# Queries, keys and rotary keys of the attention kept in DRAM as high and low parts

## The chip, the cores and the metric

The kernel runs on one core of a Trainium2 chip: a matrix engine (TensorE, PE), three others that compute (VectorE or DVE, ScalarE or ACT, GpSimd or POOL), one that mostly issues transfers (SyncE or SP), and 16 DMA engines between DRAM and the core's memory. Each engine works through its own list of instructions in order; semaphores tie the lists together. The metric is the device time of one execution in microseconds (us), smaller is better.

## What is computed

One layer of a diffusion backbone over 512 latent and 256 context tokens of width 2,048. The input projection's columns feed two groups of heads: latent attention, and a bidirectional RWKV-7 recurrence. Then one output projection and a mixture of 32 experts. The change concerns three results of the projection that the attention reads much later:

```
h = modulate(x, norm_attn_g, sh1, sc1)
cq, ckv, kr, r, k, v, wl, al, gl = project_in(h, w_in, shift_mu)
q  = rms_norm(cq,  q_norm_g)  @ w_uq        # cq: 512 wide, 512 tokens
kv = rms_norm(ckv, kv_norm_g) @ w_ukv       # ckv: 256 wide, 768 tokens
k_rope = rope_2d(kr)                        # kr: 64 wide, 768 tokens
g = sigmoid(gl) @ gate_up                   # gate of the RWKV output
```

Matrix products are taken in three passes over operands that are split into a high part (a cast to a shorter format, `fp32r`) and a low part (what is left), so that the sum has nearly float32 precision.

## The kernel before

`layer` is one long program whose instructions a scheduler orders by priority; buffers come from pools, and a pool's memory can be given to the next one only when everything that reads or writes it is done. DMAs raise one of eight semaphore slots, dealt in turn to the DMAs of SP and ACT together; a DMA that gets a slot first waits until the DMA that had it before has landed. So the order in which DMAs are scheduled ties the queues of SP and ACT to each other.

The stages, by the profile's clock: modulation and the first projection columns (to about 155 us); the other projection columns with the norms of queries and keys, the rotation of the rotary key and the gate (to about 294); the RWKV features, feature block by feature block and direction by direction (300 to 880), with POOL solving small triangular systems in the background (`solve`, whose results go out as `r_tt` and `r_tn` on SP); from 820 on the attention (`mla`), interleaved with the recurrence's chain; routing; and from about 1,690 the experts, whose weights stream in.

What the change touches:

- L384 to L400 normalise the queries `cqT` and store them, four DMAs to `r_cq` (float32). L426 to L443 do it for the keys `ckvT` in two ranges of tokens, four DMAs to `r_ckv`. L444 and L445 rotate and store `krT` to `r_kr`.
- Between them L409 to L425 load `gate_up` and split it and the gate's inputs into buffers named `ld`, of which there are three; the loop L446 to L455 forms the gate and stores it, eight DMAs to `r_g`.
- All this lies in the pool `p0` on one side of the memory. When it closes, the RWKV stage's buffers take its place: first the memset of `W` (L551), then `km`, `ks` and others.
- In `mla`, L986 to L989 load the seven pieces on ACT's queue into four buffers `p` and split each: a cast on ACT (L170) and a subtraction on DVE (L171), into `ckn`, `krr` and `cqn`. Behind them on ACT's queue come the weights of the first pair of heads (`load_pair`, L997, L998, L1003, L1004), the copy `p<-pqr` (L1015) of the first rotary queries, and its rotation.

`split(hi, lo, src)` is `sc.copy(hi, src)` and `ve.tensor_sub(lo, src, hi)`.

Of the kernel before, what the change touches and what calls it, by code (L numbers as in the profile page):

```python
# [21 lines left out]
T = 512  # L22
# [58 lines left out]
def layer(ctx, tc, tab, x, c, ctx_in, c_ctx, w_mod, b_mod, norm_attn_g, norm_ffn_g, w_in, shift_mu,  # L81
# [25 lines left out]
    r_cq = dram.tile([4, 128, T], F32, name="r_cq")  # L107
    r_ckv = dram.tile([2, 128, NT], F32, name="r_ckv")
    r_kr = dram.tile([128, NT], F32, name="r_kr")
# [176 lines left out]
    with tc.tile_pool(name="p0", bufs=1, side="right") as p0:  # L286
# [97 lines left out]
        for src, n, dst, g, width, a, b in ((cqT, 4, r_cq, qg, 512.0, 0, 512),):  # L384
            m = b - a
            pn = bank("nq", [128, 512], "rw", 2)[:, 0:m]
            for i in range(n):
                sc.activation(nsq[:, 0:m], src[:, i, a:b], AF.Square)
                te.matmul(pn, ones, nsq[:, 0:m], start=(i == 0), stop=(i == n - 1))
            v, r, u = nv[:, 0:m], nr[:, 0:m], nu[:, 0:m]  # L390
            ve.tensor_scalar(v, pn, 1.0 / width, EPS, op0=OP.mult, op1=OP.add)
            sc.activation(r, v, AF.Sqrt)
            ve.reciprocal(r, r)
            ve.tensor_mul(u, r, r)
            ve.tensor_mul(u, u, v)
            ve.tensor_scalar(u, u, -0.5, 1.5, op0=OP.mult, op1=OP.add)
            ve.tensor_mul(r, r, u)
            for i in range(n):
                ve.scalar_tensor_tensor(src[:, i, a:b], src[:, i, a:b], g[:, i:i + 1], r, op0=OP.mult, op1=OP.mult)
                sy.dma_start(dst[i, :, a:b], src[:, i, a:b])  # L400
# [25 lines left out]
        for src, n, dst, g, width, a, b in ((ckvT, 2, r_ckv, kvg, 256.0, 0, 512),  # L426
                                            (ckvT, 2, r_ckv, kvg, 256.0, 512, 768)):
# [13 lines left out]
            for i in range(n):  # L441
                ve.scalar_tensor_tensor(src[:, i, a:b], src[:, i, a:b], g[:, i:i + 1], r, op0=OP.mult, op1=OP.mult)
                sy.dma_start(dst[i, :, a:b], src[:, i, a:b])  # L443
        rope(krT[:, 0:T], "rw", 2, nsq)  # L444
        sy.dma_start(r_kr, krT)  # L445
        for f in range(NF):  # L446
# [8 lines left out]
            sy.dma_start(r_g[f], g_)  # L455
        early = [project([(3904, 128)], 128)]
# [517 lines left out]
    def mla():  # L974
        with tc.tile_pool(name="mla", bufs=1) as ml:
# [9 lines left out]
            for dst, src, n in ([([t_[:, i] for t_ in ckn], r_ckv[i], NT) for i in range(2)] + [(krr, r_kr, NT)] +  # L985
                                [([t_[:, i] for t_ in cqn], r_cq[i], T) for i in range(4)]):  # L986
                t_ = mt("p", [128, NT], bufs=4)[:, 0:n]
                sc.dma_start(t_, src)
                split(dst[0], dst[1], t_)  # L989
# [700 lines left out]
```

## Time and profile before

| | us |
|---|---|
| time, median of 3 runs | 2669.04 (2664.29 to 2672.88) |
| the profiled execution | 2665.13 |
| its span, first to last instruction | 2663.3 |
| PE busy | 2411.0 (91%) |
| DVE busy | 1406.2 (53%) |
| ACT busy | 914.1 (34%) |
| POOL busy | 737.8 (28%) |
| mean TensorE clock granted, share of full | 0.948 |

The profile shows one execution. Its page gives each engine's busy time and, in 40 slices of 66.6 us, busy tenths; the trace can be asked for an engine's timeline (start, duration, engine, line, operation, output<-input; in brackets how long the engine sat idle before and what released it), for busy times by stretch, and for transfers. A line starting with `SPq` or `ACTq` is a DMA being issued, not moved.

### The profile page before, as it was taken

What the parts mean: (1) busy time and instruction counts of PE and PEld (TensorE: products, weight loads), DVE (VectorE), ACT (ScalarE), POOL (GpSimd) and SP (SyncE); (2) the same over time, 40 slices, a digit from 0 to 9 for tenths busy, and PEclk for the clock granted to TensorE, in tenths of its full rate; (3) what the DMA queues carried; (4) which work ended last, traced back from release to release, by engine and by line L of the source; (5) the groups of instructions that cost most, each with busy time, mean ns of one, the idle gap of its engine ahead of it and who ended that gap; (6) DMA issues with size and microseconds to landing.
All of it is one profiled execution on the core that took longest, in us unless ns stands there. A gap on an engine that the chain in (4) does not pass through costs nothing. (4 is left out here: it accounts for less than half of the span.)

```text
span 2663.3 us, 39444 instructions
## 1 busy us (share of the span) xinstructions
PE 2411.0 (91%) x15238; PEld 1535.9 (58%) x15238; DVE 1406.2 (53%) x2094; ACT 914.1 (34%) x1659; POOL 737.8 (28%) x830
## 2 busy tenths in 40 slices
PE   4999899998997789998968997999999999999995
PEld 2567678887876667777736785434333334334332
DVE  3345687666778767666458545243333334334324
ACT  4245564332333256554534332311111112112202
POOL 1046654016677544554535300000000000000000
PEclk9999999998997789999989997999999999999998
DMA  8965577665667768788687532999999999999995
GB/s 307 345 189 173 190 195 185 135 141 131 150 136 183 175 180 224 223 243 237 189 271 216 193 131 106 411 421 421 421 421 420 418 421 420 420 416 417 420 421 212
DMA packets 521998, 727.50 MB, mean 273 GB/s; under 512 B 320792, under 2 KB 399536, under 8 KB 471376
## 3 DMA queue, kind: packets, MB, share of 16 engines
q1 hardware_dynamic: 410512, 578.97, 62.0%
q0 software_dynamic: 24208, 83.50, 9.5%
q10 hardware_dynamic: 87088, 62.48, 8.1%
q8 instruction: 121, 1.98, 0.3%
q14 instruction: 69, 0.57, 0.1%
HBM read 659.69 MB, written 73.54 MB: 275 GB/s over the span
## 5 line engine op out<-in xcount | busy, mean ns | idle before, releaser
L523 POOL TENSOR_TENSOR scr<-scr 128x512 f32<-128x512 f32 x240 | 327.7, 1365 | 350.5 <-ACT scr L521 331.2
L174 PE MATMUL acc<-hT,w 128*128 128x512 f32 (+1 forms) x752 | 268.7, 357 | 13.0 <-DVE km L276 9.9
L175 PE MATMUL acc<-hT,w 128*128 128x512 f32 (+1 forms) x752 | 268.9, 358 | 0.0
L176 PE MATMUL acc<-hT,w 128*128 128x512 f32 (+1 forms) x752 | 268.3, 357 | 0.0
L1455 POOL DMA_INDIRECT xg<-r_x,ix x16 | 19.1, 1196 | 831.1 <-DVE sp L1440 627.3
L521 ACT ACTIVATE scr<-scr,scl 128x512 f32<-128x512 f32 x256 | 170.4, 715 | 174.8 <-DMA scr<-in_w_mod_dram 140.6
L1600 PE MATMUL py<-ew,gT 128*64 128x512 f32 x680 | 213.8, 607 | 7.9 <-ACT gT L1580 6.7
L1500 DVE TENSOR_TENSOR xm<-xm,pox 128x512 f32<-128x512 f32 x256 | 161.4, 682 | 62.1 <-PE pox L1499 61.5
L171 DVE TENSOR_TENSOR w<-wraw,w 128x512 fp32r<-128x512 f32 (+1 forms) x132 | 110.8, 845 | 140.8 <-ACT w L170 139.7
L1575 DVE SCALAR_TENSOR_TENSOR scr<-ph,ga,scr 128x512 f32<-128x512 f32 x16 | 12.0, 751 | 310.4 <-PE ph L1556 310.4
L1490 DVE TENSOR_TENSOR yt<-py,g2r 128x512 f32<-128x512 f32 x64 | 42.7, 687 | 242.1 <-PE py L1600 228.7
L174 PEld LDWEIGHTS acc<-hT,w 128*128 128x128 f32 (+1 forms) x752 | 144.5, 192 | 36.2 <-issue 15.4
L176 PEld LDWEIGHTS acc<-hT,w 128*128 128x128 f32 (+1 forms) x752 | 143.9, 191 | 22.4 <-issue 1.4
L175 PEld LDWEIGHTS acc<-hT,w 128*128 128x128 f32 (+1 forms) x752 | 144.5, 192 | 20.4 <-issue 1.0
L170 ACT CAST w<-wraw 128x512 fp32r<-128x512 f32 (+1 forms) x132 | 80.5, 613 | 217.7 <-PE acc L175 125.3
L1600 PEld LDWEIGHTS py<-ew,gT 128*64 128x64 f32 x680 | 73.5, 138 | 125.7 <-issue 109.2
L519 POOL DMA_DIRECT2D scr<-in_w_mod_dram x128 | 92.9, 726 | 173.7 <-DVE scr L358 140.7
L170 ACT CAST yr<-yt 128x512 fp32r<-128x512 f32 x64 | 39.3, 619 | 294.3 <-DVE yt L1490 293.0
L479 POOL TENSOR_TENSOR scr<-scr 128x31 f32<-128x31 f32 (+15 forms) x155 | 108.5, 700 | 27.7 <-DMA scr<-r_ab 16.0
L480 POOL TENSOR_TENSOR scr<-scr 128x31 f32<-128x31 f32 (+15 forms) x155 | 108.1, 697 | 12.1
L1498 PE MATMUL pox<-yr,ohT 128*128 128x512 f32 x256 | 105.6, 428 | 4.1 <-ACT yr L170 3.8
L1572 ACT ACTIVATE scr<-ph 128x512 f32<-128x512 f32 x16 | 9.6, 597 | 260.2 <-PE ph L1556 260.2
(702 smaller groups left out, 5381.9 us busy)
## 6 DMA issues: line engine op xcount, KB each, us to landing
ew<-in_w_dram SPq DMA_DIRECT2D x279, 1024.0 KB, 19.8
Y<-in_w_dram SPq DMA_DIRECT2D x70, 1024.0 KB, 19.5
scr<-in_w_mod_dram POOLq DMA_DIRECT2D x128, 512.0 KB, 5.3
scr<-in_w_dram SPq DMA_DIRECT2D x34, 1024.0 KB, 19.8
ld<-in_w_mod_dram SPq DMA_DIRECT2D x32, 1024.0 KB, 7.3
wraw<-in_w_in_dram ACTq DMA_DIRECT2D x104, 256.0 KB, 3.5
wor<-in_w_out_dram ACTq DMA_DIRECT2D x64, 256.0 KB, 3.3
QXr<-r_qx SPq DMA_DIRECT2D x24, 512.0 KB, 6.0
```

What stands on the lines that cost most here:

```text
L170: sc.copy(hi, src)
L171: (lo_eng or ve).tensor_sub(lo, src, hi)
L174: te.matmul(out, lhs[0], rhs[0], start=first, stop=False)
L175: te.matmul(out, lhs[0], rhs[1], start=False, stop=False)
L176: te.matmul(out, lhs[1], rhs[0], start=False, stop=last)
L479: e.tensor_mul(z, xs.to_broadcast([128, n, m]), ms.to_broadcast([128, n, m]))
L480: e.tensor_add(xo, xo, z)
L521: sc.mul(wt[:, k] if kt + k else macc, wt[:, k], scl[:, kt + k:kt + k + 1])
L523: gp.tensor_add(macc, macc, wt[:, k])
L1498: te.matmul(po, ohT[0:np_, 128 * i:128 * i + 128], yr[0], start=True, stop=False)
L1500: ve.tensor_add(xm[:, i, ns], xm[:, i, ns], po)
L1600: te.matmul(pys[n][64 * e:64 * e + 64], gT[:, j, 64 * e:64 * e + 64], ws[e][:, n], start=(j == 0), stop=(j == 3))
```

## The change

`r_cq`, `r_ckv` and `r_kr` get a leading dimension of two. A new function `keep` splits a whole tensor into two of the `ld` buffers and stores both with one DMA each: the queries right after their norm, the keys and the rotary key behind the gate loop. `mla` loads the parts straight into the buffers that the matmuls read: six DMAs, no split. The bytes stored and the bytes loaded both double, from 2.2 to 4.4 MB.

```diff
-        for src, n, dst, g, width, a, b in ((cqT, 4, r_cq, qg, 512.0, 0, 512),):
+        for src, n, g, width, a, b in ((cqT, 4, qg, 512.0, 0, 512),):
...
-                sy.dma_start(dst[i, :, a:b], src[:, i, a:b])
+
+        def keep(dst, src):
+            hl = [p0.tile([128, 4, 512], F32R, name="ld", bufs=3) for _ in range(2)]
+            hl = [t_.rearrange("p a b -> p (a b)")[:, 0:src.shape[-1]] for t_ in hl]
+            split(hl[0], hl[1], src)
+            for q_ in range(2):
+                sy.dma_start(dst[q_], hl[q_].bitcast(F32))
+
+        keep(r_cq.rearrange("i p k n -> i p (k n)"), cqT.rearrange("p k n -> p (k n)"))
...
-                sy.dma_start(dst[i, :, a:b], src[:, i, a:b])
         rope(krT[:, 0:T], "rw", 2, nsq)
-        sy.dma_start(r_kr, krT)
...
             sy.dma_start(r_g[f], g_)
+        keep(r_ckv.rearrange("i p k n -> i p (k n)"), ckvT.rearrange("p k n -> p (k n)"))
+        keep(r_kr, krT)
         early = [project([(3904, 128)], 128)]
...
-            for dst, src, n in ([([t_[:, i] for t_ in ckn], r_ckv[i], NT) for i in range(2)] + [(krr, r_kr, NT)] +
-                                [([t_[:, i] for t_ in cqn], r_cq[i], T) for i in range(4)]):
-                t_ = mt("p", [128, NT], bufs=4)[:, 0:n]
-                sc.dma_start(t_, src)
-                split(dst[0], dst[1], t_)
+            for dst, src in ((ckn, r_ckv), (krr, r_kr), (cqn, r_cq)):
+                for i in range(2):
+                    sc.dma_start(dst[i].bitcast(F32), src[i])
```

The scheduler orders the program anew around it. Three places follow, each before and after; in brackets the semaphores that an instruction waits for (`DMAHW0` to `DMAHW7` are the eight slots). Line numbers of after are 6 or 7 higher from the gate loop on.

SP's queue at the end of the projection pool, before:

```order
L443 DMA r_ckv<-xT 128x256 [waits DMAHW0_49,DVE_49]
L443 DMA r_ckv<-xT 128x256 [waits DMAHW1_49,DVE_49]
L455 DMA r_g<-xT 128x512 [waits DMAHW3_49,DVE_49]
L455 DMA r_g<-xT 128x512 [waits DMAHW4_49,Activation_49]
L455 DMA r_g<-xT 128x512 [waits DMAHW6_49,DVE_49]
L455 DMA r_g<-xT 128x512 [waits DMAHW7_49,Activation_49]
L455 DMA r_g<-xT 128x512 [waits DMAHW1_49,DVE_49]
L455 DMA r_g<-xT 128x512 [waits DMAHW2_49,Activation_49]
L567 DMA Y<-in_decay_up_dram 64x2x128 [waits DMAHW4_49,DMAHW3_49,DMAHW5_49,DMAHW2_49,DMAHW6_49,DMAHW1_49,DMAHW7_49,DMAHW0_49,PE_49]
```

and after (the load `Y<-in_decay_up` is the first of the next stage):

```order
L460 DMA r_g<-xT 128x512 [waits DMAHW0_49,Activation_49]
L460 DMA r_g<-xT 128x512 [waits DMAHW1_49,DVE_49]
L406 DMA r_ckv<-ld 128x1536 [waits DMAHW3_49,Activation_49]
L460 DMA r_g<-xT 128x512 [waits DMAHW4_49,Activation_49]
L406 DMA r_kr<-ld 128x768 [waits DMAHW5_49,Activation_49]
L406 DMA r_ckv<-ld 128x1536 [waits DMAHW6_49,DVE_49]
L406 DMA r_kr<-ld 128x768 [waits DMAHW0_49,DVE_49]
L574 DMA Y<-in_decay_up_dram 64x2x128 [waits DMAHW4_49,DMAHW3_49,DMAHW5_49,DMAHW2_49,DMAHW6_49,DMAHW1_49,DMAHW7_49,DMAHW0_49,PE_49]
```

The four stores of keys and rotary key stand around and behind the last gate row instead of ahead of six of them. On DVE the subtraction for the last store waits for slot `DMAHW3`, the landing of the first `r_ckv` store, because it writes into that store's buffer.

ACT's queue where POOL's first solve ends (its stores `r_tt` stand in SP's queue), before:

```order
L272 ACTIVATE rs<-acc,mself 128x512 [waits DMAHW0_49,PE_49]
L253 DMA wraw<-in_w_in_dram 128x4x128 [waits DMAHW2_49,DVE_49]
L669 COPY L<-pq 128x1024 [waits PE_49]
L253 DMA wraw<-in_w_in_dram 128x4x128 [waits DMAHW4_49,DVE_49]
L669 COPY L<-pq 128x512 [waits PE_49]
L610 ACTIVATE Y<-pl,half 128x768 [waits PE_49]
```

and after:

```order
L253 DMA wraw<-in_w_in_dram 128x4x128 [waits DMAHW5_49,DVE_49]
L272 ACTIVATE rs<-acc,mself 128x512 [waits PE_49]
L676 COPY L<-pq 128x1024 [waits PE_49]
L253 DMA wraw<-in_w_in_dram 128x4x128 [waits DMAHW7_49,DVE_49]
L676 COPY L<-pq 128x512 [waits PE_49]
L617 ACTIVATE Y<-pl,half 128x768 [waits PE_49]
```

The order is nearly the same; the slots are others. Before, `DMAHW2` was last held by the third of the stores `r_tt` of that solve. After, `DMAHW5` was last held by an earlier weight load of ACT itself and `DMAHW7` by a store `r_ab` that stands ahead of `r_tt` in SP's queue.

ACT's queue where POOL's fourth solve ends, at the start of the attention, before:

```order
L610 ACTIVATE Y<-pl,half 128x768 [waits PE_49]
L997 DMA wraw<-in_w_uq_dram 128x4x128 [waits DMAHW7_49,DVE_49]
L1015 COPY p<-pqr 128x512 [waits PE_49]
L998 DMA wraw<-in_w_uq_dram 128x4x64 [waits DMAHW1_49]
L610 ACTIVATE Y<-pl,half 128x768 [waits PE_49]
L997 DMA wraw<-in_w_uq_dram 128x4x128 [waits DMAHW3_49]
L998 DMA wraw<-in_w_uq_dram 128x4x64 [waits DMAHW5_49]
L618 ACTIVATE W<-Y 128x12x64 [waits DVE_49]
```

and after:

```order
L625 ACTIVATE W<-Y 128x12x64 [waits DVE_49,Activation_49]
L626 ACTIVATE iW<-Y 128x768
L627 COPY wcs<-W 128x12 [waits Activation_49]
L1009 DMA wraw<-in_w_ukv_dram 128x2x128 [waits DMAHW6_49,DVE_49]
L1010 DMA wraw<-in_w_ukv_dram 128x2x128 [waits DMAHW0_49]
L1009 DMA wraw<-in_w_ukv_dram 128x2x128 [waits DMAHW2_49]
L1010 DMA wraw<-in_w_ukv_dram 128x2x128 [waits DMAHW4_49]
L1021 COPY p<-pqr 128x512 [waits PE_49]
```

Before, the first three loads take slots of stores that stand ahead of the solve's, and only the fourth (`DMAHW5`) one of its `r_tt`; the copy `p<-pqr` is past by then and `W` stands behind. After, the four loads of `w_ukv` take slots of two `r_tt` stores, an `r_l` store behind them and the first `r_tn`, and the copy stands behind all four; `W` is ahead.

## Rows read from the trace of the kernel before

**Rows 1.** The page, busy tenths in 40 slices of the span, two engines.
```profile
PE   4999899998997789998968997999999999999995
...
DMA  8965577665667768788687532999999999999995
```

**Rows 2.** Timelines of ACT and PE near 148 us: start, us, instruction.
```profile
146.74 1.04 ACT L417 CAST ld<-ld 32x1024 fp32r<-32x1024 f32 x1
...
148.45 2.36 PE L319 MATMUL pm<-sel,junk 128*128 128x2 f32 x16 [1.49 <-ACT junk L315]
```

**Rows 3.** Busy us by engine in one stretch (clock, DMA share, GB/s last).
```profile
200.00:280.00 80.00, 74.92 (x383) 60.99 (x382) 46.69 (x53) 40.76 (x67) 51.42 (x46) 0.98 0.62 189
```

**Rows 4.** Timelines of SP, DVE and PE at the end of the pool.
```profile
276.49 10.20 SPq L455 DMA_DIRECT2D r_g<-xT  x6
...
294.55 0.72 DVE L551 MEMSET W<- 128x792 f32 x1 [1.93 <-DMA r_g<-xT]
...
303.27 0.77 PE L174 MATMUL acc<-hT,w 128*128 128x512 f32 x1 [9.87 <-DVE km L276]
```

**Rows 5.** Transfers: stores at 266 to 270 us (to landing), total at 274 to 300.
```profile
r_ckv<-xT SPq DMA_DIRECT2D x2, 256.0 KB, 2.5
...
DMA packets 4755, 6.31 MB, mean 243 GB/s; under 512 B 417, under 2 KB 2980, under 8 KB 4754
```

**Rows 6.** Timelines of ACT, PE and SP where POOL's first solve ends.
```profile
639.83 1.01 ACT L669 COPY L<-pq 128x1024 f32<-128x1024 f32 x1 [7.55 <-DMA r_tt<-scr]
...
640.90 0.79 PE L607 MATMUL pl<-wah,uph 128*128 128x512 f32 x1 [8.32 <-ACT L L669]
...
636.30 1.25 SPq L485 DMA_DIRECT2D r_tt<-scr  x3
```

**Rows 7.** POOL's timeline: third solve's last load, fourth solve's start, middle, end.
```profile
736.22 0.49 POOL L466 DMA_DIRECT2D scr<-r_ab  x1 [19.87 <-DMA r_ax<-AX]
...
803.05 0.23 POOL L479 TENSOR_TENSOR scr<-scr 128x31 f32<-128x31 f32 x1 [3.84 <-DMA scr<-r_ab]
...
823.78 1.17 POOL L479 TENSOR_TENSOR scr<-scr 128x256 f32<-128x256 f32 x1
...
854.76 2.59 POOL L483 COPY scr<-scr 128x1024 f32<-128x1024 f32 x1
```

**Rows 8.** Busy us by engine (PE, PEld, DVE, ACT, POOL) at the attention's start.
```profile
820.00:860.00 40.00, 26.00 (x121) 20.32 (x121) 39.97 (x46) 15.21 (x25) 35.22 (x38) 0.70 0.82 201
```

**Rows 9.** DVE's timeline: the subtractions of the seven loaded pieces.
```profile
829.96 2.25 DVE L171 TENSOR_TENSOR ckn<-p,ckn 128x768 fp32r<-128x768 f32 x2
832.13 1.42 DVE L171 TENSOR_TENSOR krr<-p,krr 128x768 fp32r<-128x768 f32 x1
833.47 1.11 DVE L171 TENSOR_TENSOR cqn<-p,cqn 128x512 fp32r<-128x512 f32 x1
...
842.76 2.96 DVE L171 TENSOR_TENSOR cqn<-p,cqn 128x512 fp32r<-128x512 f32 x3
```

**Rows 10.** Timelines of ACT and SP where POOL's fourth solve ends.
```profile
850.67 0.58 ACT L1015 COPY p<-pqr 128x512 f32<-128x512 f32 x1 [1.90 <-DVE wk L171]
...
857.76 0.84 ACT L618 ACTIVATE W<-Y 128x768 f32<-128x768 f32 x1 [5.63 <-DMA r_tt<-scr]
...
857.64 2.63 SPq L486 DMA_DIRECT2D r_tn<-scr  x6
```

**Rows 11.** Timelines of PE and ACT: transposes, first query projection, end of it.
```profile
840.73 2.79 PE L668 MATMUL pq<-k_ident,BK 128*128 128x128 f32 x12 [0.97 <-DVE BK L663]
...
858.82 0.80 PE L174 MATMUL pqn<-cqn,wq 128*128 128x512 f32 x1 [1.65 <-DVE p L282]
...
863.90 0.58 ACT L170 CAST qn<-pqn 128x512 fp32r<-128x512 f32 x1 [4.46 <-PE pqn L176]
```

**Rows 12.** DVE's timeline at the last direction, and busy us by engine afterwards.
```profile
875.79 0.69 DVE L650 TENSOR_TENSOR AX<-pa,k_mask 128x512 f32<-128x512 f32 x1 [1.26 <-PE pa L649]
...
900.00:960.00 60.00, 40.80 (x165) 30.26 (x164) 47.40 (x103) 17.61 (x35) 30.11 (x46) 0.72 0.70 186
```

More of the change, by code (lines that the diff above doesn't have):

```diff
@@ L106, in layer @@
     r_g = dram.tile([NF, 128, T], F32, name="r_g")
-    r_cq = dram.tile([4, 128, T], F32, name="r_cq")
-    r_ckv = dram.tile([2, 128, NT], F32, name="r_ckv")
-    r_kr = dram.tile([128, NT], F32, name="r_kr")
+    r_cq = dram.tile([2, 128, 4, T], F32, name="r_cq")
+    r_ckv = dram.tile([2, 128, 2, NT], F32, name="r_ckv")
+    r_kr = dram.tile([2, 128, NT], F32, name="r_kr")
     r_sg = dram.tile([16, 128], F32, name="r_sg")
@@ L425, in layer @@
         ve.tensor_sub(gs[32:64, 2], g1[64:96], gs[64:96, 2])
-        for src, n, dst, g, width, a, b in ((ckvT, 2, r_ckv, kvg, 256.0, 0, 512),
-                                            (ckvT, 2, r_ckv, kvg, 256.0, 512, 768)):
+        for src, n, g, width, a, b in ((ckvT, 2, kvg, 256.0, 0, 512), (ckvT, 2, kvg, 256.0, 512, 768)):
             m = b - a
```

## The prediction

> **What bounds the kernel now.** I read the busy slices first. TensorE (PE) is at 7 to 9 tenths from the second slice on, 6 in one, and from slice 26 on the DMA engines are full as well while expert weights stream [rows 1]. That stream starts when the stages before it are done and runs at its own rate, so what they gain or lose moves the end by as much. So I looked for PE idle in the stages that the change touches, by the list of PE's waits, and followed each wait on the timelines. Four places count, in the order of the run: the rotary/gate weights near 148 us, the end of the projection pool near 294 us, one 8 us hole near 632 us, and the start of attention near 820 to 880 us. Times below are those of the trace of before.
>
> **1. Gate weights, near 148 us.** The gate weight is loaded into the same three `ld` buffers that `keep(r_cq)` now takes first, so its splits leave this place. Here they cost something: the copy `junk<-pm` on ScalarE (ACT) stands behind the 1.04 us casts, and PE waits 1.49 us for it [rows 2]. Gain 1.5 us (0 to 1.5).
>
> **2. The new split of the queries and the moved splits, 200 to 280 us.** One cast and one subtraction of 2,048 elements, estimated at twice the 1,024 cast of 1.04 us [rows 2], 2.1 us on ACT and somewhat more on VectorE (DVE), and the gate casts moved here. PE is busy 74.9 of 80 us, DVE 46.7 and ACT 40.8 [rows 3], so about 35 us of room on each covers 5 us of new work. I take 0; if the cover failed on one engine the price would be its 2.1 us.
>
> **3. The end of the projection pool, near 294 us.** The first RWKV buffers lie where the pool was; the memset of `W` waits until the last DMA out of it has landed, at 294.55, although the last gate row was issued by 286.7 [rows 4]. PE then sits idle 9.87 us until the chain memset, `km`, shift has run [rows 4]. Before, the keys were stored ahead of the last six gate rows; now 2.36 MB (2 x 786 KB and 2 x 393 KB) leave at the end of the gate loop, and the low half of the rotary key waits for a buffer that the high half of the keys must first have left. The bounds: at the speed of the quick rows (256 KB in 2.5 us [rows 5]) the high half's landing, a subtraction of 1.4 us [rows 9] and the low half's landing end at 286.7 + 2.5 + 1.4 + 2.5 = 293.1, so 0. At the speed of the last gate row (256 KB issued by 286.7, landed 294.55, 7.9 us [rows 4]) it is 286.7 + 7.9 + 1.4 + 1.5 x 7.9 = 307.9, so +13.3. I take the mean rate of that stretch, 243 GB/s [rows 5]: 2.36 MB is 9.7 us from 286.7, and one landing of 4.2 us, between the two rows, makes 300.6. PE's wait grows by 6.0.
>
> By the Trainium skill (DMA: Bandwidth & Descriptors, Anatomy of one DMA) a transfer costs about 2.0 us and its bytes at 436 GB/s; 256 KB would be 2.6 us, near the quick rows and a third of the slow one, and step 3 would then cost nothing.
>
> **4. The hole at 632 us.** PE waits 8.32 us for the copy `L`, and ACT had been idle 7.55 us before it, released by the DMA `r_tt` [rows 6]. ACT stands at a weight load that needs a semaphore slot last used by the third `r_tt` store, and SyncE (SP) can issue that store only when GpSimd's (POOL's) first solve ends, at 636.30 [rows 6]. The excerpt of SP's and ACT's order shows that this coupling goes: with other DMAs ahead, the round of slots is another, and ACT's loads ahead of both `L` copies now wait for stores ahead of `r_tt`. The first PE instruction that hangs on this solve's stores comes 140 instructions later than before. Gain 8.3; bound 0 if a similar slot takes its place. The gain is not lost on POOL: its third solve sits idle 19.87 us for stores of this stage (736.22 [rows 7]), so it starts as much sooner as the stage runs ahead.
>
> **5. Attention's start, 820 to 880 us.** What goes: seven subtractions on DVE, 2.25 + 1.42 + 1.11 + 2.96 = 7.7 us [rows 9], and their casts. DVE has no idle here at all, 39.97 of 40 us, and PE is busy 26 of 40 [rows 8]; taken alone this is worth up to 7.7 us. What is late next: in the new order of ACT the four loads of `w_ukv` stand ahead of the copy `p<-pqr`, and they take slots of `r_tt`, of `r_l` and of `r_tn`, that is of POOL's fourth solve. Before, that copy ran at 850.67, and only `W` was held by `r_tt`, 5.63 us, with DVE busy meanwhile [rows 10]. Now the copy must wait until the first `r_tn` (issued 857.64 [rows 10], with two `r_l` stores ahead of it now) has landed: about 862. PE's next instruction in order, `pw`, waits for that copy, and behind it stand 12 `pq` transposes (2.79 us), 12 `pqn` matmuls (858.82 to 863.90, 5.1 us) [rows 11] and then the last direction's `pa`, some 2 us: 862 + 0.6 + 1.1 + 2.8 + 5.1 + 2 = 873.6, against the store of that direction's `AX` at 875.79 before [rows 12]. So of 7.7 us only about 2 are left. Then POOL: its solve took 803.05 to 823.78 for the first half and until 854.76 for the second, whose widths mirror the first [rows 7]: 20.7 against 31.0 us. Of the 10.3 us more, a quarter (7.7 of the 31 us in which DVE worked) is 2.5 us that the splits no longer take. Against both, the first head's scores come later, by some 14 us, as the queries' rotation now follows 862; PE is idle 19.2 of 60 us between 900 and 960 [rows 12], into which most of that work can move. The doubled loads (2.2 MB more at 201 GB/s [rows 8], 11 us) end near 843, and the `pqr` matmuls then follow work that runs to 844; were they late, the wait at 862 would hide it. I take -3 for the place: bounds -7.7 (no hold) and +14 (nothing of the late head absorbed).
>
> By the Trainium skill (SBUF — State Buffer, two separate sides) DVE and GpSimd share a port pair that one instruction holds whole, a DVE operation with two SBUF inputs among them. The mirrored halves agree with a contest; a full block for every split is more than their 10.3 us over 31 show. By it POOL would get back all 7.7 us.
>
> **Sum.** -1.5 + 0 + 6.0 - 8.3 - 3 = -6.8 us. The profiled execution took 2665.13 (span 2663.3 and 1.83 around it), so 2658.3 for it; the median of the runs shown is 2669.04, 3.9 above, and I forecast on the median: 2662.2. A measurement of this kernel tells about 0.3%, 8.0 us, from no change, so the likeliest outcome is a gain at the edge of what can be seen.
>
> **Rivals.**
> - *The pool's end is free.* The stores go at 2.5 us for 256 KB, [rows 5], step 3 is 0: -12.8, 2656.2. For it: that row has the same queue and source. Against: the last gate row, a few us from the place, took three times as long [rows 4].
> - *Another hole for the one at 632.* The scheduler deals slots afresh everywhere; a load before a DVE or PE need may now wait for another store of a solve. Step 4 is 0: +1.5, 2670.5. For it: place 5 is just this. Against: at the second and third solve's end I followed the slots through both orders, and the first PE instruction that hangs on them is the same one.
> - *Slower: the copy `p<-pqr` behind POOL's solve.* At 862 PE stands at `pw`, in order, with everything of the first head behind it. If the idle of 900 to 960 takes none of the 14 us, step 5 is +14 and the sum +10.2: 2679. It is slower by more than 0.3% once about 12 of the 14 stay. Against: the hole in 900 to 960 is larger than 14.
> - *POOL gets all 7.7 us.* A split holds POOL for its whole length. Then `r_tn`, and with it the copy and PE behind it, come 5.2 us sooner than in step 5: -12.0, 2657. Against: 10.3 us of excess over 31 us of a full DVE is a third, not the whole. The lock of the State Buffer page, above, would do this.
>
> **How the numbers follow.** The forecast as summed 0.40; pool's end free 0.17; another hole 0.20; slower copy 0.15; POOL's lock 0.08. Faster by over 0.3% holds the pool's end and the lock (0.25) and the part of the forecast's case beyond -8, about 0.15: 0.40. Slower holds the late copy but for a fifth of it: 0.12. Within 0.3%: 0.48. The range runs from 2651, where a free end and a part of the lock meet, to 2676, short of the full late head; some 2 in 10 lie outside.
>
> **What would show it.** PE's wait for `km` near 300 should be 14 to 18 us, 9.87 if step 3 is nothing. The wait of `pl` for `L` near 632 should be gone, and no wait over 3 us in its place before 820. ACT should stand idle before `p<-pqr` until a landing of `r_tn` about 862 minus the shift, with PE idle at `pw`. POOL's fourth solve should be about 2.5 us shorter. The forecast is wrong if the hole at 632 is there still, if the pool's end costs over 12 us, or if PE's idle from 880 to 960 grows by as much as it is idle at `pw`.

## The result: 18 us slower, and where they are

| | before | changed |
|---|---|---|
| median, us | 2670.64 (8 runs) | 2688.72 (8 runs) |
| ratio to before, 95% interval | | 1.0076 [1.0055, 1.0096] |
| the profiled execution, us | 2665.13 | 2683.51 |

I had forecast 2662.2 with a range to 2676. So the forecast is wrong in its sign, and the time lies outside the range.

The two rows of the page that answer to [rows 1], of the changed kernel, and its TensorE clock in tenths of full speed:

```profile
PE   4998799999998779999967897999999999999995
PEclk9999899999997789999989997999999999999998
DMA  9956667656667678788786633899999999999995
```

In the fifth slice (267 to 334 us) PE fell from 8 to 7 tenths, while the DMA engines went from 5 to 6. From slice 26 on all is as before, only later.

**A table by stage.** One pair of profiles is not enough here: the kernel before was profiled a second time and came out 4.5 us longer (2669.63), the changed one 9.4 us longer (2692.90). So I set the same PE instructions of each trace beside those of the first profile of before (the shift of a stage's border is the median over the matching instructions within 15 us of it). The program of before up to 815 us also stands in the experiments e2 and e9 (and up to 625 in e6), that of the changed kernel in e1. Means over the profiles that share a program, us against the first profile of before, with each one's value:

| stage | program of before | changed program | difference | forecast |
|---|---|---|---|---|
| 0 to 140 | -0.6 (0, 0.1, -1.8, -1.0, -0.5) | 0.0 (1.0, -0.2, -0.9) | +0.6 | |
| 140 to 292 | 1.0 (0, -0.1, 0.8, 1.5, 2.9) | 2.1 (2.9, 1.2, 2.1) | +1.1 | -1.5 |
| 292 to 318, pool's end | 0.0 (0, 0.2, -0.4, 0.7, -0.4) | 10.2 (10.7, 10.0, 10.1) | **+10.2** | +6.0 |
| 318 to 490 | -0.6 (0, -1.6, 0, 1.3, -2.7) | 2.4 (0.5, 3.4, 3.4) | +3.0 | |
| 490 to 625 | 4.7 (0, 5.4, 3.9, 3.9, 10.1) | 4.6 (4.6, 4.7, 4.6) | -0.1 | |
| 625 to 650, the hole | 1.5 (0, 3.3, 1.3, 1.3) | -8.3 (-8.3, -8.3, -8.5) | **-9.8** | -8.3 |
| 650 to 815 | 2.1 (0, 0, 4.2, 4.2) | 7.3 (7.1, 7.0, 7.7) | **+5.2** | |
| 815 to 905 | -2.3 (0, -4.6) | 3.0 (3.2, 2.8) | **+5.3** | -3 |
| 905 to 1,500 | -0.7 (0, -1.4) | 2.0 (-3.2, 7.2) | +2.7 | |

The differences add to 18.2 us; the medians are 18.1 apart. The last two rows rest on two profiles each: in 815 to 905 the two of before differ by 4.6 us, and the last row moves by 10 us between two executions of one program.

**The pool's end.** Timelines of the changed kernel from 288 to 318 us (start, us, instruction; in brackets the idle before it and what ended it); it answers to [rows 4]:

```profile
290.10 0.32 SPq L406 DMA_DIRECT2D r_ckv<-ld  x1
...
292.56 0.93 SPq L406 DMA_DIRECT2D r_ckv<-ld  x1
302.62 0.32 SPq L406 DMA_DIRECT2D r_kr<-ld  x1
...
299.17 1.33 ACT L528 ACTIVATE scr<-scr,scl 128x512 f32<-128x512 f32 x2 [7.88 <-DMA scr<-in_w_mod_dram]
300.40 0.60 ACT L170 CAST w<-wraw 128x512 fp32r<-128x512 f32 x1
...
301.04 0.69 DVE L171 TENSOR_TENSOR w<-wraw,w 128x512 fp32r<-128x512 f32 x1 [8.51 <-ACT w L170]
301.65 0.95 DVE L171 TENSOR_TENSOR ld<-xT,ld 128x768 fp32r<-128x768 f32 x1
...
305.85 0.72 DVE L558 MEMSET W<- 128x792 f32 x1 [2.27 <-DMA r_kr<-ld]
...
312.76 1.33 ACT L528 ACTIVATE scr<-scr,scl 128x512 f32<-128x512 f32 x2 [4.60 <-DMA scr<-in_w_mod_dram]
314.00 0.81 ACT L170 CAST uph<-Y 64x256 fp32r<-64x256 f32 x2
...
317.19 0.77 PE L174 MATMUL acc<-hT,w 128*128 128x512 f32 x1 [19.88 <-DVE km L276]
```

PE stands 19.88 us instead of 9.87. The low half of the rotary key is stored at 302.62 and lands some 3 us later, so the place is the one that I named. But what it waited for is not what I named. DVE stands 8.51 us at a weight split that is ahead of the subtraction in its queue; ACT's half of that split stands behind a step of the background modulation (`scr`, L528), and that step waits 7.88 us for its weights, a 512 KB load on POOL's queue. Further on the same happens to `uph` and with it to `km`: another 4.60 us. The landing that I had named, of the first `r_ckv` store, came at 295.29, before anything waited for it.

The same step stood in the way before the change, for a shorter time. Timelines of ACT and DVE before:

```profile
290.06 1.34 ACT L521 ACTIVATE scr<-scr,scl 128x512 f32<-128x512 f32 x2 [3.71 <-DMA scr<-in_w_mod_dram]
...
291.94 0.69 DVE L171 TENSOR_TENSOR w<-wraw,w 128x512 fp32r<-128x512 f32 x1 [6.08 <-ACT w L170]
```

From issue to landing the two loads at this place took 5.3 and 8.0 us before, 8.2 and 10.7 in the changed kernel. So the loads are slower by about 3 us each beside the stores; the rest of the longer waits lies in when they are issued and in the order of the queues, which I have not taken apart.

**The hole.** Waits of PE by releaser, changed kernel, 630 to 670 us; it answers to [rows 6]:

```profile
PE pl L614 <- ACT L L676: 1.1, 1, 1.1
```

8.32 has become 1.1. The coupling is gone, as the order had shown.

**The attention's start.** Timelines of the changed kernel where POOL's fourth solve ends; they answer to [rows 7] and [rows 10]:

```profile
815.77 0.24 POOL L486 TENSOR_TENSOR scr<-scr 128x31 f32<-128x31 f32 x1 [2.88 <-DMA scr<-r_ab]
...
868.00 2.00 POOL L490 COPY scr<-scr 128x1024 f32<-128x1024 f32 x1
...
872.06 4.81 SPq L493 DMA_DIRECT2D r_tn<-scr  x6
...
876.29 0.59 ACT L1021 COPY p<-pqr 128x512 f32<-128x512 f32 x1 [10.79 <-DMA r_tn<-scr]
...
876.93 2.08 PE L281 MATMUL pw<-p,k_swap 128*128 128x512 f32 x2 [2.44 <-ACT p L1021]
...
895.63 0.80 PE L174 MATMUL sp<-kn,qn 128*128 128x512 f32 x1 [5.57 <-ACT kn L170]
```

ACT stands 10.79 us until an `r_tn` store has landed. The stage enters 18.4 us late, so on the clock of before the copy is at 857.9, 4 us ahead of my 862 and 7.2 behind the 850.67 of before. PE stands 2.44 us at `pw` and 5.57 at the first scores, in the second profile 2.60 and 4.82; before it stood at neither.

### The profile page after: what moved, and what is told of

It reads as the page before. It is cut to its first block, busy times and chain, and to the rows that moved or that the text cites. A ratio compares the mean times of both kernels' runs of the same rounds, so it can differ in the third digit from the quotient of the medians.

```text
span 2681.6 us, 39441 instructions
## 1 busy us (share of the span) xinstructions
PE 2418.4 (90%) x15238; PEld 1537.9 (57%) x15238; DVE 1423.9 (53%) x2090; ACT 916.3 (34%) x1657; POOL 742.1 (28%) x830
## 5 line engine op out<-in xcount | busy, mean ns | idle before, releaser
L528 ACT ACTIVATE scr<-scr,scl 128x512 f32<-128x512 f32 x256 | 170.7, 715 | 149.5 <-DMA scr<-in_w_mod_dram 133.3
L1504 PE MATMUL pox<-yr,ohT 128*128 128x512 f32 x256 | 105.1, 426 | 4.1 <-ACT yr L170 3.8
L1505 PE MATMUL pox<-yr,ohT 128*128 128x512 f32 x256 | 98.4, 401 | 0.1
```

What stands on the lines that cost most here:

```text
L528: sc.mul(wt[:, k] if kt + k else macc, wt[:, k], scl[:, kt + k:kt + k + 1])
L1504: te.matmul(po, ohT[0:np_, 128 * i:128 * i + 128], yr[0], start=True, stop=False)
```

## Experiments

All ratios are to the kernel before, measured on the same chip. "Changed" is the changed kernel.

### The two sides of the change apart

**e1**: changed, but read as before from the high parts.

```diff
-            for dst, src in ((ckn, r_ckv), (krr, r_kr), (cqn, r_cq)):
-                for i in range(2):
-                    sc.dma_start(dst[i].bitcast(F32), src[i])
+            for dst, src, n in (... r_ckv[0][:, i] ..., (krr, r_kr[0], NT), ... r_cq[0][:, i] ...):
+                t_ = mt("p", [128, NT], bufs=4)[:, 0:n]
+                sc.dma_start(t_, src)
+                split(dst[0], dst[1], t_)
```

> The write side of the change alone: the parts are made and stored as in the changed kernel, the attention loads the high parts as seven pieces and splits them on reading as before (the stored low parts are not read, so the values are those of the high parts). Up to 820 us the program is that of the changed kernel. Theory (the loss is made where the parts are stored, and the attention gives nothing back): PE stands 18 to 20 us at the end of the projection pool, 9.9 before; no hole at 632 us; the run is 12 to 22 us slower than before, ratio 1.005 to 1.008. Rival (the loss is in the attention, where the copy p<-pqr stands behind POOL's solve): this kernel does not have that order, so ratio 0.997 to 1.002.

Measured: 2698.85 us, 1.0103 [1.0071, 1.0135]. PE's wait for `km` is 19.91 us and the hole is gone, as expected; at 815 us this kernel is 18.6 us behind the first profile of before, as the changed one is (18.4). Against the mean of the traces with the program of before that is some 10 us, so by the table above the write side makes a little over half of the loss. From 815 on e1 loses 16 us more, 7 of them by 905. The copy `p<-pqr` does not stand behind the loads of `w_ukv` here, as I had said, but the coupling is there all the same, at the cast behind the fourth of them:

```profile
872.80 0.40 ACT L170 CAST wk<-wraw 128x256 fp32r<-128x256 f32 x1 [10.10 <-DMA r_tt<-scr]
...
874.06 3.78 PE L656 MATMUL pa<-Q,BK 64*128 64x128 f32 x16 [7.07 <-ACT Y L617]
```

So the rival's mechanism is not excluded by this run. What is lost behind 905 neither theory had.

**e2**: stored as before, read as in the changed kernel (both parts from one array).

```diff
-                    sc.dma_start(dst[i].bitcast(F32), src[i])
+                    sc.dma_start(dst[i].bitcast(F32), src[0])
```

> The read side of the change alone: the results are stored once and unsplit as before, the attention loads six whole tensors and splits nothing (the same stored array is read for the high and for the low part, so the low part is not the remainder). Theory (the attention's seven subtractions are worth little, because other waits stand behind them): pool's end and the hole of 8.3 us at 632 us as before, ratio 0.998 to 1.001. Rival (the reads are the gain that the stores then lose): 7.7 us less of DVE work at its full stretch, ratio 0.996 to 0.998. Rival (the doubled loads cost): ratio over 1.002.

Measured: 2683.57 us, 1.0056 [1.0034, 1.0078]. The number is that of the last rival, the place is not. Beside the second profile of before, whose program is the same to 820 us, e2 is 0.7 us later at 820 to 830, again 0.7 or less between 940 and 960, and then 13 to 16 us later at 1,240 to 1,330, where no load or split of the change stands. Busy times by engine (PE, PEld, DVE, ACT, POOL; then clock, DMA share, GB/s), second profile of before, and e2:

```profile
1030.00:1330.00 300.00, 280.67 (x4663) 225.45 (x4665) 185.65 (x309) 164.73 (x323) 157.79 (x150) 0.96 0.82 230
```

```profile
1030.00:1330.00 300.00, 278.12 (x4401) 221.73 (x4402) 186.46 (x301) 155.86 (x306) 155.34 (x145) 0.93 0.80 225
```

PE is busy as long and does 262 matmuls fewer: the granted clock is 0.93 instead of 0.96, and the heads and the recurrence's chain are interleaved in another order. So for the first heads the missing subtractions are worth nothing, and what costs lies behind them; whether it is the order or the clock, this pair does not tell. The first scores come at 887.68 here, 11 us behind that profile of before on the same clock, although no copy is held: a late first head does not need the hold.

**e3 and e4**: only the queries, only the keys and rotary keys, kept in parts; the rest stored and read as before.

```diff
-        keep(r_ckv...)                                  # e3; e4 leaves out keep(r_cq...)
-        keep(r_kr, krT)
+                sy.dma_start(r_ckv[0][:, i, a:b], src[:, i, a:b])
+        sy.dma_start(r_kr[0], krT)
```

> Only the queries are kept in parts, stored early and loaded in parts; keys and rotary keys go as before. Theory: PE's wait at the pool's end is about 10 us as before, the new split of 2,048 elements costs 2 to 4 us between 200 and 250 us because it stands ahead of weight splits in the queues of ACT and DVE, and the hole at 632 us goes (no weight load ahead of the copies L takes a slot of the solve's stores), 8 us: ratio 0.996 to 0.999. Rival (the loss of the changed kernel lies in a TensorE clock or order of the later stages that any new order brings): ratio 1.002 to 1.006.

> Only the keys and rotary keys are kept in parts, behind the gate loop; the queries go as before. Theory (the pool's end makes the loss): PE waits 18 to 20 us for km near 300 us; in this order the weight loads ahead of the copies L take no slot of the first solve's stores, but the second of two later ones does, ahead of the first feature's Y<-pl, so that the hole at 632 us is moved and not surely gone: ratio 1.003 to 1.007. Rival (the queries' split makes the loss): ratio 0.998 to 1.001.

Measured: e3 2681.95, 1.006 [1.0033, 1.0087]; e4 2711.10, 1.0163 [1.013, 1.0196]. e3: the pool's end costs 2.4 us and the hole is gone, so at 815 us it is 1.9 us behind the first profile of before and some 6 ahead of the mean of its traces, as I had expected; then 13 us are lost behind, 7 to 8 of them by 905, where the copy stands behind the four loads of `w_ukv` again:

```profile
870.54 0.58 ACT L1025 COPY p<-pqr 128x512 f32<-128x512 f32 x1 [22.19 <-DMA wraw<-in_w_ukv_dram]
...
871.17 2.07 PE L281 MATMUL pw<-p,k_swap 128*128 128x512 f32 x2 [11.60 <-ACT p L1025]
```

e4: PE stands 21.74 us at the pool's end, somewhat more than expected, but another 27 us are lost, some 13 to 15 of them between 490 and 625; I have not followed why. The keys make the pool's end; neither half keeps its gain.

### The pool's end

**e5**: the changed kernel with memory of their own for the parts of keys and rotary keys. `keep2` writes the high part where it is told and forms the low part in place.

```diff
-        keep(r_ckv.rearrange(...), ckvT.rearrange(...))
-        keep(r_kr, krT)
+        keep2(r_ckv.rearrange(...), ckvT.rearrange(...), cqT.rearrange("p k n -> p (k n)")[:, 0:2 * NT])
+        keep2(r_kr, krT, carve(NT))
```

> The changed kernel, but the parts of keys and rotary keys do not share the three ld buffers: the high parts go where the stored queries lay and into a free piece of the same tile, the low parts are formed in place, so no part waits for the landing of another and the scheduler puts all four stores among the gate rows. Theory (the wait at the pool's end is the two landings and what is queued between them): PE's wait for km near 300 us falls from 19.9 to 9 to 12 us, the time by 8 to 11 against the changed kernel, ratio to before 1.002 to 1.005. Rival (the bytes of the doubled stores make it): the wait stays over 16 us and the ratio at 1.006 to 1.009.

Measured: 2670.26 us, 0.9993 [0.997, 1.0017], 0.8% below the changed kernel (1.0076). PE's wait, by the timeline:

```profile
299.70 0.76 PE L174 MATMUL acc<-hT,w 128*128 128x512 f32 x1 [6.12 <-DVE km L276]
```

6.12 is below the 9.87 of before. The same bytes, stored earlier between the gate rows, cost nothing: at 318 us e5 stands between level with the first profile of before and 3 us ahead of it, by how the instructions are matched, where the changed kernel is 11 to 15 behind. So the rival falls. The time came down by more than I had expected: another 4 to 7 us are gained between 318 and 490, and for these I have no cause.

**e7**: own memory for the rotary key alone, so that no store waits for another's landing.

```diff
-        keep(r_kr, krT)
+        keep2(r_kr, krT, carve(NT))
```

> The changed kernel, but only the rotary key's parts have memory of their own (high part in a free piece, low part formed in place); the keys' parts use the ld buffers behind the gate loop as in the changed kernel. So 1.6 MB still leave at the very end, but nothing waits for a landing before its own store. Theory (at the pool's end it is the chain landing, subtraction, landing and what stands in DVE's queue between them): PE's wait for km is 11 to 15 us, between 9.9 of before and 19.9 of the changed kernel. Rival (the bytes): 17 us or more. In this order a weight load ahead of the first copy L takes a slot of the first solve's stores again, so the hole near 632 us must be back with about 8 us; ratio to before 1.003 to 1.009.

Measured: 2707.40 us, 1.0148 [1.0115, 1.018]. The hole is back with 7.11 us, as expected. At the pool's end my theory missed: 17.88 us is in the rival's range, and the total lies above the one that I had given. Timelines:

```profile
298.06 1.33 ACT L535 ACTIVATE scr<-scr,scl 128x512 f32<-128x512 f32 x2 [3.19 <-DMA scr<-in_w_mod_dram]
...
299.94 1.36 DVE L171 TENSOR_TENSOR w<-wraw,w 128x512 fp32r<-128x512 f32 x1 [4.34 <-ACT w L170]
301.41 0.72 DVE L565 MEMSET W<- 128x792 f32 x1
...
312.48 0.77 PE L174 MATMUL acc<-hT,w 128*128 128x512 f32 x1 [17.88 <-DVE km L276]
```

Without the second landing, and with the two `r_kr` stores gone from the end as well (they left near 268), PE waits 2.0 us less, of the 10. `W` waits for no store any more: DVE comes to it only after a weight split that stands behind the modulation on ACT.

**e11**: the changed kernel without the modulation in that stretch.

```diff
-NM = (6, 0, 0)
+NM = (0, 0, 0)
```

> The changed kernel, with the six quarters of modulation that ACT and POOL work off in the background of the projections moved to after the recurrence's features; no other edit. Same four stores in the same places at the pool's end. Theory (the store burst makes the loads of modulation weights late, and ACT's and DVE's splits, which the pool's end and km need, stand behind them): PE's wait for km falls from 19.9 us to 9 to 13. Rival (the landings of the stores themselves): 16 us or more. The total says nothing, since the moved quarters lengthen a later stage; 1.00 to 1.03.

Measured: 2778.85 us, 1.0425 [1.0384, 1.0466] (the moved quarters run later with nothing beside them). The pool's end, timelines:

```profile
283.71 0.72 DVE L558 MEMSET W<- 128x792 f32 x1 [0.41 <-DMA r_kr<-ld]
...
290.69 0.77 PE L174 MATMUL acc<-hT,w 128*128 128x512 f32 x1 [8.64 <-DVE km L276]
```

With the same four stores in the same order, `W` waits 0.41 us for the last of them and PE 8.64 us for `km`. So the landings do not make the 19.88 us: with the modulation the in-order queues of ACT and DVE hand its delay to the splits behind. Not shown is that the stores cost nothing at all. No run takes the modulation out of the kernel before, whose 9.87 us hold a part of the same delay; and without the modulation ACT has less work and the DMA engines fewer bytes.

### The hole, and what any new order costs

**e6**: the kernel before, the results of the solves on POOL's own queue.

```diff
-                    drain(solve_p(sy, e, *SOLVES[f // 2 - 1]))
+                    drain(solve_p(gp, e, *SOLVES[f // 2 - 1]))
```

> The kernel before, with one thing moved: the results of POOL's first solves go out on POOL's own queue instead of SP's, so that no store that waits for a solve takes a semaphore slot that a weight load on ACT's queue gets next. Nothing is kept in parts. Theory (the hole at 632 us is that coupling and its 8.3 us reach the end): the PE wait for L near 632 us is gone, ratio 0.995 to 0.998. Rival (a gain before 820 us is given back where the attention and the recurrence's chain are interleaved, which any new order disturbs): the hole is gone, but ratio 0.999 to 1.006.

Measured: 2677.72 us, 1.0027 [1.0001, 1.0054]. The wait of 8.3 us is 1.0 and the stage 625 to 650 is 11.9 us shorter, yet the kernel is not faster. In its profile, which came out 13 us above the median of its runs, some 15 to 18 us are lost between 905 and 1,500. The rival's number holds; its place only in part, for by 1,340, where heads and chain have ended, e6 is 6 us behind the first profile of before, and by 1,500 it is 20.

**e9**: the kernel before, reading the seven pieces in another order.

```diff
-            for dst, src, n in (... ckn ... + [(krr, r_kr, NT)] + ... cqn ...):
+            for dst, src, n in (... cqn ... + [(krr, r_kr, NT)] + ... ckn ...):
```

> The kernel before with the seven pieces read in another order (queries, rotary key, keys); the same work to the last instruction, nothing kept in parts. Theory (the order of before between 815 and 1,500 us is one that other orders do not reach, so that almost any edit there costs): same program to 820 us, then 5 to 15 us slower, ratio 1.002 to 1.006. Rival (reading in parts has a cost of its own): ratio 0.998 to 1.002.

Measured: 2673.24 us, 1.0015 [0.9996, 1.0035]; neither theory is excluded. This new order alone costs less than the 15 us of e2.

**e10**: own memory as in e5, read as before from the high parts (the edit of e1 in e5).

> The write side with own memory, and the read side as before (the high parts are read as seven pieces and split on reading; the stored low parts are not read). Against the kernel with own memory and parts read it shows what reading in parts is worth when the rest is alike. Theory (it is worth nothing or costs): within 0.3% of that kernel's 0.9993 or below it. Rival (it is worth its 7.7 us of DVE work): 1.002 to 1.005.

Measured: 2674.39 us, 1.003 [1.0006, 1.0054]. The number is in the rival's range: reading in parts is worth 4 us by the medians, 10 by the two ratios. But the intervals of e5 and e10 overlap, and e2 says the opposite. It stays open.

**e8**: e5 and e6 together.

> Own memory for the parts of keys and rotary keys, and the solves' results on POOL's own queue; no load of weights takes a slot of a solve's store anywhere before 900 us. Theory (the copy p<-pqr at the start of the attention is late because four weight loads ahead of it take such slots): ACT's idle of 12.5 us before that copy and PE's 7.1 us at pw are gone, and the stretch 815 to 905 us is 5 to 9 us shorter than with own memory alone; ratio to before 0.993 to 0.998. Rival (what is gained by 905 us is lost by 1,500 us in the interleave of heads and chain): the same at 905, but ratio 0.998 to 1.004.

Measured: 2667.89 us, 0.9991 [0.9969, 1.0014]. Timelines at the copy that was late, of e5 and of e8:

```profile
851.11 0.59 ACT L1029 COPY p<-pqr 128x512 f32<-128x512 f32 x1 [12.54 <-DMA wraw<-in_w_ukv_dram]
...
851.75 2.07 PE L281 MATMUL pw<-p,k_swap 128*128 128x512 f32 x2 [7.06 <-ACT p L1029]
```

```profile
848.14 0.58 ACT L1029 COPY p<-pqr 128x512 f32<-128x512 f32 x1 [4.18 <-DMA wraw<-in_w_ukv_dram]
...
850.19 1.12 PE L281 MATMUL pw<-p,k_swap 128*128 128x512 f32 x2
```

With the hold PE waits 7.06 us at `pw` and 3.19 at the first scores, without it at neither; the stage 815 to 905 takes 9.3 us more than before in e5 and 4.7 less in e8. So of 14 us between these two traces 10 are waits that the hold explains, and it is the mechanism of my slower rival.

At 1,000 us the heads of e8 are 11 to 13 us ahead of the first profile of before, but the recurrence's chain beside them is between level and 3 us behind: what I had called a lead of 12 us is one of the heads alone. When heads and chain have both ended, near 1,330 us, e8 is 10 us ahead all the same, and by 1,500 it is level or 4 behind. So the lead is not lost in the interleave but behind it, where the output projection (`po_s`), the last norms of the recurrence's output (`rov`) and the rows of the modulation (`prr`) follow. Two of PE's waits from 1,315 to 1,520 us, before and e8:

```profile
PE po_s L175 <- DVE wo L171: 2.3, 1, 2.3
PE prr L1120 <- DVE g1r L1121: 1.9, 1, 1.9
```

```profile
PE po_s L175 <- DVE wo L171: 11.4, 2, 6.7
PE prr L1134 <- ACT g1r L1135: 11.2, 1, 11.2
```

One wait of before, 13.1 us of `po_s` for a weight, is all but gone in e8, but the seven longest groups of waits there add to 50.7 us in e8 and 37.2 before. Why they are longer no run shows.

**e12 and e13**: e8 with seven quarters of modulation ahead of the attention, and e8 with 9 instead of 12 steps of attention ahead of the last solves.

```diff
-NM = (6, 0, 0)
+NM = (7, 0, 0)      # e12
-NFILL = 12
+NFILL = 9           # e13
```

> Own memory, the solves' results on POOL's queue, and seven instead of six quarters of modulation ahead of the attention, so that less of it stands in the stretch 900 to 1,500 us. Theory (what own memory and the freed hole win is lost in the interleave of heads and chain, since ACT, DVE and POOL carry the modulation there as well): 3 to 8 us faster than that kernel without this, ratio to before 0.995 to 0.998. Rival (the interleave follows the order, not the load): 0.998 to 1.004.

> Own memory, the solves' results on POOL's queue, and 9 instead of 12 steps of the attention ahead of the last solves: the same work in another interleave. Theory (the interleave sets what is left of the 12 us that this kernel has won by 1,000 us): a change of 3 to 12 us in either sign, all of it after 900 us. Rival (the end of that stage is bound elsewhere): within 2 us of 2,668.

Measured: e12 2666.67, 0.9994 [0.9971, 1.0017]; e13 2688.04, 1.0079 [1.0049, 1.0109]. Both theories missed: one quarter less changes nothing, and another interleave of the same work costs 20 us by the medians, more than I had allowed. So the order of the work behind 900 us can be worth as much as the whole loss of the changed kernel. No kernel beat the one before beyond its interval; e5, e8 and e12 are level with it and 0.8% below the changed one.

### Second profiles

> The kernel before once more, for a second profile. Theory (at the same instructions TensorE's clock falls in one execution and not in another, so the stretches at 500 and 720 us in which the changed kernel ran at the lower clock are no part of the change): of the stretches of 20 us between 400 and 820, other ones than in the first profile show a granted clock below 0.95, with 2 to 8 us more or less until 820. Rival (the clock follows the order): the same stretches, at 420, 640 and 760, and 820 is reached within 1 us of the first.

> The changed kernel once more, for a second profile. Theory (the falls of the clock are not tied to the order): the stretches near 515 and 728 us are not both at the lower clock again. Rival (they belong to the order): both again, 0.83 and 0.74, and the wait for km 19.9 us in either case within 0.5.

The same instructions, first and second profile of before, then of the changed kernel (columns as in [rows 3]):

```profile
490.00:530.00 40.00, 38.73 (x223) 31.78 (x222) 30.16 (x39) 17.57 (x26) 0.49 (x1) 1.00 0.76 162
```

```profile
490.00:530.00 40.00, 39.33 (x194) 32.17 (x193) 25.10 (x37) 16.13 (x24) 0.49 (x1) 0.83 0.73 157
```

```profile
490.00:530.00 40.00, 39.34 (x201) 31.49 (x201) 29.88 (x44) 12.87 (x21) 0.00 (x0) 0.87 0.62 126
715.00:745.00 30.00, 28.45 (x143) 23.03 (x144) 23.03 (x33) 9.64 (x15) 9.01 (x17) 0.83 0.86 189
```

```profile
490.00:530.00 40.00, 39.34 (x202) 31.73 (x201) 29.87 (x45) 12.72 (x19) 0.00 (x0) 0.87 0.63 131
715.00:745.00 30.00, 28.39 (x142) 22.81 (x142) 23.20 (x32) 9.63 (x15) 8.52 (x16) 0.83 0.89 195
```

For before the theory held: in 490 to 530 us PE ran at 2.4 GHz throughout in one profile and for a third of the time at 1.2 GHz in the other (0.83), and that stage took 5.4 us more. For the changed kernel it missed: both falls came again. In 715 to 745 PE had just waited 1.55 us for `L`, against 0.67 in before. e5 and e10, whose programs are the same to 820 us, show the pair once more: a wait of 0.71 us at that place and full clock, a wait of 2.02 us and a fall to 1.2 GHz; the stage 650 to 815 differs by 9.7 us between them. Timelines of PE there, of e5 and of e10:

```profile
705.45 0.49 PE L622 MATMUL pl<-wah,uph 128*128 128x512 f32 x1 [0.71 <-ACT L L684]
705.87 0.50 PE L623 MATMUL pl<-wal,uph 64*128 64x512 f32 x1
```

```profile
706.53 0.51 PE L622 MATMUL pl<-wah,uph 128*128 128x512 f32 x1 [2.02 <-ACT L L684]
706.98 0.79 PE L623 MATMUL pl<-wal,uph 64*128 64x512 f32 x1
```

In e10 PE ran 17.1 us at 1.2 GHz there, from 706.9; at half the clock that loses some 8.5 us, by my estimate, and with 1.3 us more of waiting this is about the difference of 9.7. The wait is not shown to be the cause. After waits of 1.55 us or more the clock fell in all seven traces that have one (changed, its second profile, e1, e4, e8, e10, e13), for 10 to 17 us; but after a wait of 0.66 or 0.67 us it fell too in e2, e6, e7, e9 and e12, mostly for 7 us, and did not in the two profiles of before.

## Why the prediction was wrong, step by step

1. **Gate weights.** The wait of 1.49 us for `junk` is gone, as forecast.
2. **Queries' split at 0.** This step failed. PE's waits in 140 to 292 are 11.2 to 12.5 us in the traces without this split and 12.9 to 15.5 in those with it, e11 aside. Of these 2.4 to 4.2 us are waits for a weight split on DVE, and there is none without it. Timelines of the changed kernel:

```profile
213.30 1.90 ACT L170 CAST ld<-xT 128x2048 fp32r<-128x2048 f32 x1 [3.11 <-DVE xT L399]
...
215.24 2.29 DVE L171 TENSOR_TENSOR ld<-xT,ld 128x2048 fp32r<-128x2048 f32 x1 [1.50 <-ACT ld L170]
217.44 1.63 DVE L171 TENSOR_TENSOR w<-wraw,w 128x384 fp32r<-128x384 f32 x1
...
219.13 0.47 PE L176 MATMUL acc<-hT,w 128*96 128x512 f32 x1 [0.93 <-DVE w L171]
```

   The durations were as estimated (1.90 and 2.29 us), and the engines had the room. But the cast waits 3.11 us for its input at the head of ACT's queue, and the weight splits that PE needs next stand behind it on both engines. I read room from busy shares where the order decides. In e11, which has this split but no modulation beside it, no such wait is left, so here too it is the two together. Steps 1 and 2 together came to +1.1 instead of -1.5.
3. **Pool's end at +6.0.** Right place and sign, and in that partly luck: the term was +10.2, inside my upper bound of +13.3, but the chain that I had summed is not the one that PE waited for. I priced the bytes and a landing. What the runs show is a weight split behind a step of the modulation that waits for its own load (7.88 and 8.51 us on ACT and DVE, 3.71 and 6.08 before); without the second landing the wait is 2.0 us shorter (e7), without the modulation 11.2 (e11). The Trainium skill (DMA: Bandwidth & Descriptors, Anatomy of one DMA) would have had the step at 0, by the transfers alone. Its fit is for DMAs that GpSimd issues, these are SP's: it gives 2.9 us for the 384 KB of a part of `r_kr` and 3.8 for the 768 KB of a part of `r_ckv`, as estimates. The last `r_kr` store, alone, landed in 2.9 us; the three that left together took 5.2 to 9.9.
4. **The hole at -8.3.** Right: -9.8, and no store of a solve took its place ahead of 815 us. The +5.2 of 650 to 815 is no such hole either but for the most part a fall of the clock, 10.2 us at 1.2 GHz in the changed kernel. All three of its traces have that; of the four with the program of before two have a shorter one.
5. **Attention's start at -3.** This step failed: +5.3, and the term that failed is the gain. The hold was seen: the copy came 4 us earlier than forecast, and the first scores at 895.63 were 8.6 us late on the clock of before (868.61 there), not 14. But without the hold (e2 against the second profile of before) the seven subtractions were worth under 1 us by 960, so nothing stood against the 7 to 8 us that PE stood at `pw` and at the scores. POOL's fourth solve was not 2.5 us shorter in the changed kernel: from its first step to the start of its copy it took 52.2 us, against 51.7 and 53.4 in the two profiles of before. Over all runs the term fits better: 51.7 to 53.4 us in the six traces that split all seven pieces there, 48.7 to 52.3 in the eight that split none, some 2 us apart by the means (e3 and e4, which split three and four, have 53.5 and 49.4; e11 aside). That goes the way of the Trainium skill (SBUF — State Buffer, two separate sides), by which a DVE operation with two SBUF inputs and a GpSimd operation that reads SBUF contend for a shared port; it is far from all 7.7 us, and the orders of these kernels differ as well.
6. **No term for the rest.** Against the forecast the kernel came out 25 us late: 2.6 by steps 1 and 2, 4.2 by step 3, 8.3 by step 5, less 1.5 by step 4, and 11.4 in stretches for which I had no term, nearly half of that in 650 to 815. I carried gains at 632 and 820 us to the end unchanged. The runs show that one program's traces differ by up to 10 us in a stage with the same instructions, and that a kernel 10 us ahead at 1,330 us can be level at 1,500 (e8). What makes these 11.4 us, and how much of them is chance, stays open.

Of the rivals, the slower one named a mechanism that is there, but not the main cost; it reckoned with a pool's end of +6 and took the attention's start for the hinge. The range ended 12.7 us short of the measured median.

## What to carry to other kernels

Work that fits by busy time is not hidden when it waits at the head of an in-order queue: look at what stands behind it there, and what that in turn holds. A burst of stores need not cost what its bytes suggest; look for a background loader on another queue whose late data stands ahead of foreground work. A lead in one of two interleaved chains is no lead of the kernel. In a kernel whose order a scheduler deals anew, measure an edit against a second profile and a neutral reordering before crediting it with a gain of 0.3%.

## What was not expected of the hardware

- The granted clock differs between executions at the same instructions: 1.00 and 0.83 in 490 to 530 us of before, with 5.4 us of difference in that stage.
- Seven traces with a wait of 1.55 to 3.96 us of PE ahead of the `pl` matmuls near 720 us all went on at 1.2 GHz, for 10 to 17 us; five with a wait of 0.67 us did so too, mostly for 7 us, and three with one of 0.67 to 0.71 (both profiles of before, e5) stayed at 2.4 GHz.
- Doubling the stored bytes cost nothing where the stores stood between the gate rows (e5: PE's wait 6.12 us, before 9.87, and level or ahead at 318 us).
